# A streaming-encoder block on one core: the causal mask halved and moved into the opening's pool, its memory given to third places for three kinds of tiles

## The chip, the cores and the metric

The kernel runs on one core of one Trainium2 chip. The metric is the device time of one execution in microseconds (us): the median of three timed runs. TensorE does the matmuls, VectorE (DVE) and ScalarE (ACT) the work on elements, GpSimd (POOL) some more of it, and SyncE (SP) issues most of the transfers between HBM and the on-chip memory (SBUF). An engine works through its own instructions in order.

## The reference

One layer of a block with two branches, for 1,024 tokens of width 1,024, all in float32:

```
h = rmsnorm(x, ln1_g) * (1 + sc1) + sh1
q, k, v, cb, cc, cx, ga, gb = split(h @ w_in)          # eight sections of 1024 columns
q, k = rmsnorm(q per head), rmsnorm(k per head)        # 16 heads of 64
y_a = stick_breaking_attention(q, k, v)                # strictly causal
y_b = cb * causal_dwconv3(cc * cx)
merged = sigmoid(ga) * (y_a @ w_branch_a) + sigmoid(gb) * (y_b @ w_branch_b)
x = x + g1 * (merged @ w_out)
h = rmsnorm(x, ln2_g) * (1 + sc2) + sh2
x = x + g2 * ((silu(h @ w_ffn_gate) * (h @ w_ffn_up)) @ w_ffn_down)
```

sh1, sc1, g1, sh2, sc2 and g2 come from a small product of the condition c with `ada_w`.

## The kernel before

Every float32 operand of a large product is split into a high part (a copy in the fast matmul format) and a low part (the difference), and a product is three matmuls: high by high, high by low and low by high. So nearly each weight and each activation passes ScalarE (the copy) and VectorE (the subtraction) before TensorE reads it.

The stages, in the order of the program:

- **Opening** (L313 to L417). The modulation's sums, the squares of x, and the sections v (sweep `psr`) and again v with the modulation's shift (`pss`). TensorE first warms up with matmuls on the mask `mk` (L323 to L332). The sweep over k fills six PSUM banks for the first six token tiles; the last two tiles are done by `tail(k0, k1)`. `tail(0, KB)` runs ahead of `bcast` (L383), which spreads the rows' scales over all partitions by small matmuls, and `tail(KB, KT)` runs behind it. `bcast` writes into banks that `finish_raw(0)` and `finish_raw(1)` have emptied. From L169 to L496 the order on every engine is written out: `in_order` ties each instruction to the one before it on its engine. The opening's own pool `sp` is closed at L417, and the next pool, `ap`, begins at the same place in memory; its first tile, `vs`, is written by `finish_v(pss[0], 0)` (L480).
- **Keys and factors** (L420 to L614).
- **Gates** (L745 to L816). Twenty pairs of column blocks, each done with seven products in place of eight (`g_prod`, 12 matmuls each). For the first four pairs, the queries, a finished tile c goes through `put_q`: its high and low parts are stored, it is squared, and the square is split into `sh` and `sl` in a tile `sq2` of tag `sq`. `sum_q` then adds the squares up over partitions by two matmuls (L701). `later()` is called four times a pair, between two products, and decides when: it holds finished squares back in the list `pmm`. The modulation's later sums (`mods_later`) also load into tiles of tag `sq`.
- **Attention** (L977 to L1130), with TensorE's gaps filled by branch B's products (`fillers`). The order on TensorE, and of attention's own steps on VectorE and GpSimd, is tied. `load_sb` reads the gates of branch B into tiles of tag `sgi`.
- **Branch A** (L1167 to L1206). The attention's output is read into tiles `yr` (L1173) and split into `ya` (L1176, L1177). For each of 16 tiles there are 24 matmuls (`mm_ch`, L1026 to L1028) into one of two banks `pj`; the product is multiplied by the gate `sa` of tag `sgi` (loaded at L1192, used at L1197), `mb` is added (L1198), and the result is split (L1202, L1203). The gate's place is free when L1203 is done.
- **Output, second norm and the feed-forward part** (from L1213).

Where no order is tied, a planner that simulates the engines' times orders each engine's instructions and thus also the transfers that it issues. A tag with `bufs` places holds so many tiles; the next one waits until the oldest is no longer read. Pools on the left side of the memory stand on top of each other from `const` upwards.

The mask `mk` is a 128 x 1,024 tile in the pool `const`, which lives to the end: zeros, and in the last 128 columns ones on and above the diagonal (L88 to L91). Only the warming matmuls read its second half, `mr` copies it for them, and L497 stores 512 zeros of its first row into HBM, as the row ahead of the values `d_v[1]`.

Of the kernel before, what the change touches and what calls it, by code (L numbers as in the profile page):

```python
# [9 lines left out]
F32 = mybir.dt.float32  # L10
F32R = mybir.dt.float32r
AF = mybir.ActivationFunctionType
ALU = mybir.AluOpType
# [4 lines left out]
P = 128  # L18
T = 1024
D = 1024  # L20
# [10 lines left out]
def block_kernel(tc, x, x_t, cols, ada_1, ada_2, ada_row, w_q, w_kv, w_cg, w_a, w_b, w_o, w_g, w_u, w_d, out):  # L31
    nc = tc.nc
    st = ExitStack()
    const = st.enter_context(tc.tile_pool(name="const", bufs=1, reuse_waits="tile"))
# [5 lines left out]
    def nm(s):  # L40
        uid[0] += 1
        return f"{s}_{uid[0]}"
# [12 lines left out]
    def load_w(src):  # L55
# [14 lines left out]
    d_v = [drp.tile([n, P + 1, KT, P], F32, name=f"d_v{n}_{e}") for e, n in enumerate((4, 4))]  # L70
# [14 lines left out]
    ident = const.tile([P, P], F32, name="dm")  # L85
    make_identity(nc, ident)

    mk = const.tile([P, D], F32, name="mk")  # L88
    nc.gpsimd.memset(mk, 0.0)
    nc.gpsimd.affine_select(out=mk[:, D - P:], in_=mk[:, D - P:], compare_op=ALU.is_ge, fill=1.0, base=-1,  # L90
                            pattern=[[-1, P]], channel_multiplier=1)  # L91
    one = const.tile([P, 1], F32, name="one")
    nc.vector.memset(one, 1.0)
    nc.scalar.activation(one, one, AF.Silu)
# [75 lines left out]
    s1 = ExitStack()  # L170
    sp = s1.enter_context(tc.tile_pool(name="start", bufs=1, reuse_waits="tile"))
    xts = xp.tile([P, KT, T], F32, name="xts")

    def xt(k, n=None):
        ns = slice(0, T) if n is None else slice(n * 512, n * 512 + 512)
# [22 lines left out]
    def load_ada(m, k):  # L198
        ads[m, k] = load_ring(ada_1[k][:, m])

    wq = []
    NLD, MC, NW, KB = 5, 2, 3, 2

    def load_wq(qt):
        wp, bufs = wps
# [116 lines left out]
    load_x(3)  # L322
    warm = [ps_tr() for e in range(2)]  # L323
    for e in range(NW - 1):
        nc.tensor.matmul(warm[0], ident, mk[:, 512:], start=True, stop=True)
    mr = [sp.tile([P, n], F32R, name=nm("mr")) for n in (P, 512)]
    for m_ in mr:
        nc.scalar.activation(m_, mk[:, D - m_.shape[1]:], AF.Copy)
    for whole in (1, 1, 0, 0, 1, 1, 0, 1, 1, 1, 1):
        for e in range(2 - whole):  # L330
            r = slice(0, P) if whole else slice(64 * e, 64 * e + 64)
# [70 lines left out]
    for k in range(KT - 1):  # L402
        real(pss, k, range(MC), wq[4:])
        split_lo(k + 9)
        for n in range(2):
            make_hi(k + 1, n)
            make_lo(k + 1, n)
        if k + 2 < KT:
            split_hi(k + 10)
            shift_sum(k + 2)  # L410
            norm_x(k + 2)
        real(pss, k, range(MC, 8), wq[4:])
        if k % 2 == 0:
            load_wq(k // 2 + 6)
        if k + 3 < KT:
            load_ada(0, k + 3)
    s1.close()  # L417


# [74 lines left out]
            load_wq(9 + i // 2)  # L494
            split_w(9 + i // 2)
    ends = in_order(i0)  # L496
    nc.scalar.dma_start(d_v[1][:, 0:1, 0].rearrange("r p d -> p r d"), mk[0:1, :512].rearrange("p (r d) -> p r d", d=P))  # L497

    def put_before(e):

# [129 lines left out]
    def g_big():  # L630
        return gp.tile([P, T + 2], F32, tag="uu", bufs=2, name=nm("uu"))
# [28 lines left out]
    def mods_later():  # L660

        csb, cab = g_big()[:, :D], gp.tile([P, D], F32, tag="tr", bufs=2, name=nm("cab"))
        nc.scalar.dma_start(cab, ada_row[0:1, :].broadcast_to([P, D]))
        nc.scalar.activation(csb, cab, AF.Sigmoid)
        tt(nc.vector, cab, cab, csb, ALU.mult)
        yield

        def big_(i):
            tag = ("uu", "sq", "uu", "sq", "tr")[i % 5]
            return g_big()[:, :D] if tag == "uu" else gp.tile([P, D], F32, tag=tag, bufs=2, name=nm("ad"))  # L670

        yield from mod_sums((2, 4), big_, lambda s, t_: g_tile()[:, :P], cab, nc.scalar, g_ss)

# [11 lines left out]

    def put_q(c, m, n):

        sq2, hl_ = (gp.tile([P, 2, 512], F32R, tag=t_, bufs=2, name=nm("gt")) for t_ in ("sq", "tr"))
        hi, lo, sh, sl = hl_[:, 0], hl_[:, 1], sq2[:, 0], sq2[:, 1]
        nc.scalar.activation(hi, c, AF.Identity, scale=qgc)  # L690
        nc.vector.scalar_tensor_tensor(out=lo, in0=c, scalar=qgc, in1=hi.bitcast(F32), op0=ALU.mult, op1=ALU.subtract)
        nc.scalar.activation(c, c, AF.Square)
        nc.scalar.activation(sh, c, AF.Copy)
        tt(nc.vector, sl, c, sh.bitcast(F32), ALU.subtract)
        for e, t in ((0, hi), (1, lo)):
            nc.scalar.dma_start(d_q[e][m, :, n * 512:(n + 1) * 512], t.bitcast(F32))
        pmm.append((m, n, sh, sl))
# [47 lines left out]
    for g, (sec, j) in enumerate(gates):  # L745
        raw, raw2 = raws
        p1, p2 = pre[g] if g in pre else (g_prod(g_split(raw[:, :512]), 0), g_prod(g_split(raw[:, 512:]), 1))
        a11, a12, a21, a22 = raw[:, :512], raw[:, 512:], raw2[:, :512], raw2[:, 512:]
        s1, s2_, s3, s4 = (gp2.tile([P, 512], F32, tag=f"ws{q}", bufs=1, name=nm("ws")) for q in range(4))
        with tc.high_priority() if g == 0 else ExitStack():  # L750
            tt(nc.gpsimd, s3, a11, a21, ALU.subtract)
            tt(nc.gpsimd, s2_, a22, s3, ALU.subtract)
            w6 = g_split(s2_)
        tt(nc.gpsimd, s1, a21, a22, ALU.add)
        ws4 = nc.gpsimd.tensor_tensor(out=s4, in0=a12, in1=s2_, op=ALU.subtract)
        if g + 1 < len(gates):
            raws = two_raw(g + 1)
        c11, c21, c12, c22 = (gp.tile([P, 512], F32, tag=f"c{q}", bufs=2, name=nm("c")) for q in range(4))

        def put(c, m, n):  # L760
            if sec == 5:
                pend.append((c, m, n))
            elif sec > 2:
                nc.scalar.activation(c, c, AF.Sigmoid)
                nc.scalar.dma_start((d_sga, d_sgb)[sec - 3][m, :, n * 512:(n + 1) * 512], c)
            elif sec == 1:
                ccs[m, n] = c
            elif n == 1 and m >= 4:
                ccs["late"] = c
            else:  # L770
                put_u(c, m, n)
                if n == 0 and m >= 4:
                    put_u(ccs["late"], m, 1)

        def later():
            if len(pmm) > 1 or pmm and not pend:
                sum_q(*pmm.pop(0))
            if pend:
                put_q(*pend.pop(0))
            elif g > 3 and not pmm:  # L780
                with tc.issue_after(ws4.ins):
                    next(eq, None)

        nc.scalar.activation(c11, p1, AF.Copy)
        p4 = g_prod(g_split(a22), 3) if g + 1 == len(gates) else None
        p6 = g_prod(w6, 5)
        tt(nc.vector, c21, p6, c11, ALU.add)
        tt(nc.vector, c11, p2, c11, ALU.add)
        put(c11, j, 0)
        later()  # L790
        p5 = g_prod(g_split(s1), 4)
        tt(nc.vector, c12, p5, c21, ALU.add)
        p3 = g_prod(g_split(s4), 2) if g == 0 else None
        p7 = g_prod(g_split(s3), 6)
        tt(nc.vector, c22, p7, c12, ALU.add)
        put(c22, j + 4, 1)
        later()
        tt(nc.vector, c21, p7, c21, ALU.add)
        p3 = p3 or g_prod(g_split(s4), 2)
        tt(nc.vector, c12, p3, c12, ALU.add)  # L800
        put(c12, j, 1)
        later()
        p4 = p4 or g_prod(g_split(a22), 3)
        tt(nc.vector, c21, p4, c21, ALU.add)
        later()
        put(c21, j + 4, 0)
        if g + 1 == len(gates):
            for _ in eq:
                pass
        for _ in range((3 if sec in (3, 4) else 0) if g + 1 < len(gates) else 50):  # L810
            next(ml, None)
# [218 lines left out]
    def fillers():  # L1030
# [19 lines left out]
            nc.sync.dma_start(d_yb[1][n][:, m, :], yl.bitcast(F32))  # L1050
            yield 0.65 * KQ
        def load_sb(m, n):
            sb = fp.tile([P, 512], F32, tag="sgi", bufs=2, name=nm("sgi"))
            nc.sync.dma_start(sb, d_sgb[m, :, n * 512:(n + 1) * 512])
            return sb

# [112 lines left out]
    yah, yal = ([[None] * KT for n in range(2)] for e in range(2))  # L1169
    with tc.high_priority():  # L1170
        for (tag, bufs), (n, k) in zip(slots, [(0, k) for k in range(7)] + [(1, 0), (1, 1), (1, 2), (0, 7)] + [(1, k) for k in range(3, 8)]):
            yr = fp.tile([P, 512], F32, tag="yr", bufs=2, name=nm("yr"))
            nc.sync.dma_start(yr, d_ya[n][:, k, :])  # L1173
            ya2 = bp.tile([P, 2, 512], F32R, tag=tag, bufs=bufs, name=nm("ya"))
            h_, l_ = ya2[:, 0], ya2[:, 1]
            nc.scalar.activation(h_, yr, AF.Copy)  # L1176
            tt(nc.vector, l_, yr, h_.bitcast(F32), ALU.subtract)  # L1177
            yah[n][k], yal[n][k] = h_, l_
    mh, mlo = [None] * 2, [None] * 2
    wa = {}  # L1180
    for it, (m, n) in enumerate([(0, 0), (1, 0), (0, 1), (1, 1)] + [(m, n) for m in range(2, KT) for n in range(2)]):
# [6 lines left out]
        if (m, n) == (KT - 1, 0):  # L1188
            with tc.issue_after(last_m.ins):
                preload_wo()  # L1190
        sa = fp.tile([P, 512], F32, tag="sgi", bufs=2, name=nm("sgi"))
        nc.sync.dma_start(sa, d_sga[m, :, n * 512:(n + 1) * 512])  # L1192
        mb = fp.tile([P, 512], F32, tag="st", bufs=3, name=nm("mb"))
        nc.sync.dma_start(mb, d_mb[m, :, n * 512:(n + 1) * 512])
# [596 lines left out]
```

## Time and profile before

| | |
|---|---|
| timed runs | 1797.07 us median (1796.59 to 1797.15, 3 runs) |
| the profiled execution | 1798.88 us, its span 1796.9 us |
| TensorE busy | 1784.6 us, 99% of the span |
| VectorE, ScalarE, GpSimd busy | 1272.0, 830.8, 342.9 us |
| moved by transfers | 359.09 MB, 200 GB/s on average |

A profile is one execution on the chip. A row of a timeline gives the start and the length in us, the engine, the source line, what is written and read, the shape, a count of like instructions, and in brackets how long the engine stood idle before it and what ended that. `L137` is the line of a helper, so its rows are told apart by their tiles. Matmuls are pipelined: a row's length is that of one matmul from its start to its end, and the next one starts before that. An engine named with a q (SPq, ACTq) is its sequencer, issuing a transfer. The granted clock is the share of TensorE's full clock that the throttle let through.

### The profile page before, as it was taken

To read this page: it belongs to the slowest core of one execution; us is meant where nothing else is said; L and a number is where in the kernel's file an instruction comes from. 1 tells how busy PE (TensorE), PEld (TensorE's weight loads), DVE (VectorE), ACT (ScalarE), POOL (GpSimd) and SP (SyncE) were. 2 spreads that over 40 slices of the span, in tenths; PEclk is the share of its full clock that TensorE was granted. 3 is DMA by queue.
4 is the path that set the end of the run, shared out by engine and by line. 5 is a ranking of instruction groups with operands and counts; after the bars stand their busy time and mean duration, and the time that the engine had idled before them with its cause. 6 is when DMAs were issued, how large, how long until landed. Compare 5 with 4: busy or idle time off the path is not lost.

```text
span 1796.9 us, 24937 instructions
## 1 busy us (share of the span) xinstructions
PE 1784.6 (99%) x8611; PEld 1486.4 (83%) x8611; DVE 1272.0 (71%) x2030; ACT 830.8 (46%) x1555; POOL 342.9 (19%) x437
## 2 busy tenths in 40 slices
PE   9999999999999999999999999999999999999999
PEld 7888877888888888888888788888888888888887
DVE  6876576777774678777786764698867786644776
ACT  5534364333433567766675221764544454432321
POOL 0024334723231233333342100100000000000000
PEclk9999999999999999999999999999999999999999
DMA  9469654222644977796656766334533444389776
GB/s 384 165 237 382 239 187 141 88 87 99 222 151 143 297 193 189 207 320 179 169 135 199 263 210 213 129 104 157 220 130 134 159 171 159 136 320 348 272 235 222
DMA packets 165010, 359.09 MB, mean 200 GB/s; under 512 B 15538, under 2 KB 60938, under 8 KB 163732
## 3 DMA queue, kind: packets, MB, share of 16 engines
q1 hardware_dynamic: 128300, 289.65, 48.8%
q10 hardware_dynamic: 33096, 55.25, 8.7%
q0 software_dynamic: 3488, 12.59, 2.1%
q8 instruction: 69, 1.13, 0.3%
q14 instruction: 57, 0.47, 0.1%
HBM read 247.84 MB, written 109.62 MB: 199 GB/s over the span
## 4 chain that ended last, share of the span: by engine, by line
PE 93%; DMA 3%; DVE 2%; ACT 1%; issue 1%; POOL 0%; SPq 0%; ACTq 0%; DVEq 0%; POOLq 0%
PE e L133 8%; PE e L131 8%; PE e L132 8%; PE pj L133 7%; PE pj L131 7%; PE pj L132 7%; PE pj L294 7%; PE pj L1026 4%; PE pj L1027 4%; PE pj L1028 4%; PE e L1619 4%; PE e L1618 4%; PE e L1620 4%; PE tr L950 3%; PE o L966 2%; PE z L921 2%
## 5 line engine op out<-in xcount | busy, mean ns | idle before, releaser
L1234 ACT ACTIVATE whi<-raw 128x512 fp32r<-128x512 f32 x137 | 85.0, 628 | 160.8 <-PE e L132 101.8
L1235 DVE TENSOR_TENSOR wlo<-raw,whi 128x512 fp32r<-128x512 f32 x137 | 93.2, 687 | 71.0 <-ACT whi L1234 53.5
L137 POOL TENSOR_TENSOR pt<-pt 128x63 f32<-128x63 f32 (+7 forms) x128 | 101.8, 795 | 211.7 <-DVE pt L936 188.8
L132 PE MATMUL e<-big,whi 128*128 128x512 f32 x352 | 136.9, 389 | 0.0
L131 PE MATMUL e<-big,whi 128*128 128x512 f32 x352 | 136.5, 390 | 0.0
L133 PE MATMUL e<-big,wlo 128*128 128x512 f32 x352 | 136.1, 389 | 0.0
L294 PE MATMUL pj<-whi,big 128*128 128x512 f32 x448 | 132.6, 393 | 0.5 <-ACT big L263 0.3
L137 DVE TENSOR_TENSOR c<-pj,c 128x512 f32<-128x512 f32 x140 | 93.5, 683 | 50.7 <-PE pj L133 50.2
L954 DVE TENSOR_TENSOR atl<-tr,ath 128x512 fp32r<-128x512 f32 (+1 forms) x192 | 104.0, 553 | 34.3 <-ACT ath L953 33.0
L131 PE MATMUL pj<-big,whi 128*128 128x512 f32 x320 | 125.0, 391 | 0.0
L133 PE MATMUL pj<-big,wlo 128*128 128x512 f32 x320 | 124.8, 390 | 0.0
L132 PE MATMUL pj<-big,whi 128*128 128x512 f32 x320 | 124.6, 389 | 0.0
L1619 PE MATMUL e<-wlo,f 128*128 128x512 f32 (+1 forms) x319 | 121.8, 382 | 0.0
L1618 PE MATMUL e<-whi,f 128*128 128x512 f32 (+1 forms) x319 | 121.6, 382 | 0.0
L1620 PE MATMUL e<-whi,f 128*128 128x512 f32 (+1 forms) x319 | 121.6, 382 | 0.0
L923 ACT ACTIVATE pt<-z,rq 128x128 f32<-128x128 f32 (+1 forms) x192 | 107.3, 579 | 26.3 <-PE z L922 23.3
L1026 PE MATMUL pj<-big,whi 128*128 128x512 f32 x256 | 113.2, 442 | 0.0
L137 DVE TENSOR_TENSOR wlo<-raw,whi 128x512 fp32r<-128x512 f32 x108 | 87.3, 813 | 32.4 <-ACT whi L524 32.1
L524 ACT ACTIVATE whi<-raw 128x512 fp32r<-128x512 f32 x108 | 67.3, 628 | 90.0 <-PE pj L132 51.5
L953 ACT ACTIVATE ath<-tr 128x512 fp32r<-128x512 f32 (+1 forms) x192 | 93.3, 489 | 28.5 <-PE tr L950 27.4
L131 PE MATMUL e<-rh,whi 128*128 128x512 f32 x264 | 102.7, 389 | 0.0
L132 PE MATMUL e<-rl,whi 128*128 128x512 f32 x264 | 102.7, 389 | 0.0
(304 smaller groups left out, 4760.4 us busy)
## 6 DMA issues: line engine op xcount, KB each, us to landing
f<-d_f SPq DMA_DIRECT2D x77, 512.0 KB, 4.4
d_f<-fs SPq DMA_DIRECT2D x70, 512.0 KB, 3.2
raw<-w_cg SPq DMA_DIRECT2D x40, 512.0 KB, 3.7
raw<-w_u SPq DMA_DIRECT2D x26, 512.0 KB, 4.2
raw<-w_g SPq DMA_DIRECT2D x25, 512.0 KB, 4.0
raw<-w_kv SPq DMA_DIRECT2D x20, 512.0 KB, 5.0
ld<-ada SPq DMA_DIRECT2D x16, 512.0 KB, 6.6
d_t<-ts SPq DMA_DIRECT2D x16, 512.0 KB, 6.9
```

The source lines that it names most:

```text
L131: nc.tensor.matmul(ps, wh[:, k, :], fh[:, k, :], start=(k == 0 and not onto), stop=False, skip_group_check=onto)
L132: nc.tensor.matmul(ps, wh[:, k, :], fl[:, k, :], start=False, stop=False, skip_group_check=onto)
L133: last = nc.tensor.matmul(ps, wl[:, k, :], fh[:, k, :], start=False, stop=(k == 3), skip_group_check=onto)
L137: eng.tensor_tensor(out=out, in0=a, in1=b, op=op)
L294: nc.tensor.matmul(ps, a, b, start=(k == 0 and q == 0), stop=(k == KT - 1 and q == 2))
L923: nc.scalar.activation(pt[:, off + s0:off + s0 + m], z[:, :m], AF.Sigmoid, scale=rq[:, 1, i, h:h + 1])
L953: nc.scalar.activation(th[:, :nb, c0:c0 + P], src, AF.Copy)
L954: nc.vector.tensor_tensor(out=tl[:, :nb, c0:c0 + P], in0=src, in1=th[:, :nb, c0:c0 + P].bitcast(F32), op=ALU.subtract)
L1026: nc.tensor.matmul(ps, wh, rh_, start=(k == 0), stop=False)
L1618: nc.tensor.matmul(o, sh, w[0][:, c], start=(j == 0), stop=False)
L1619: nc.tensor.matmul(o, sh, w[1][:, c], start=False, stop=False)
L1620: nc.tensor.matmul(o, sl, w[0][:, c], start=False, stop=(j == NJ - 1))
```

## The change

The mask leaves `const`, is 512 columns wide, and is made in the opening's pool `sp`; the zero row is stored at the end of the opening, before the pool closes, and so inside the stretch whose order is tied. `const` is 4 KB a partition smaller. That memory goes to a third place for tiles of tag `sq` (4 KB) in the gates' pool, and later to a third place each for `sgi` and `yr` (2 KB each) in the pool `fp`. Two counts change with it: `KB` is 3, so `tail` does three steps of k ahead of the broadcast, and `later()` holds squares back until more than two are waiting.

```
-    mk = const.tile([P, D], F32, name="mk")
-    nc.gpsimd.memset(mk, 0.0)
-    nc.gpsimd.affine_select(out=mk[:, D - P:], in_=mk[:, D - P:], compare_op=ALU.is_ge, fill=1.0, base=-1,
-                            pattern=[[-1, P]], channel_multiplier=1)
...
+    mk = sp.tile([P, 512], F32, name="mk")
+    nc.gpsimd.memset(mk, 0.0)
+    nc.gpsimd.affine_select(out=mk[:, 512 - P:], in_=mk[:, 512 - P:], compare_op=ALU.is_ge, fill=1.0, base=-1,
+                            pattern=[[-1, P]], channel_multiplier=1)
...
-    NLD, MC, NW, KB = 5, 2, 3, 2
+    NLD, MC, NW, KB = 5, 2, 3, 3
...
-        nc.tensor.matmul(warm[0], ident, mk[:, 512:], start=True, stop=True)
+        nc.tensor.matmul(warm[0], ident, mk, start=True, stop=True)
...
+    nc.scalar.dma_start(d_v[1][:, 0:1, 0].rearrange("r p d -> p r d"), mk[0:1].rearrange("p (r d) -> p r d", d=P))
     s1.close()
...
     ends = in_order(i0)
-    nc.scalar.dma_start(d_v[1][:, 0:1, 0].rearrange("r p d -> p r d"), mk[0:1, :512].rearrange("p (r d) -> p r d", d=P))
...
-            return g_big()[:, :D] if tag == "uu" else gp.tile([P, D], F32, tag=tag, bufs=2, name=nm("ad"))
+            return g_big()[:, :D] if tag == "uu" else gp.tile([P, D], F32, tag=tag, bufs=3 if tag == "sq" else 2, name=nm("ad"))
...
-        sq2, hl_ = (gp.tile([P, 2, 512], F32R, tag=t_, bufs=2, name=nm("gt")) for t_ in ("sq", "tr"))
+        sq2, hl_ = (gp.tile([P, 2, 512], F32R, tag=t_, bufs=b_, name=nm("gt")) for t_, b_ in (("sq", 3), ("tr", 2)))
...
-            if len(pmm) > 1 or pmm and not pend:
+            if len(pmm) > 2 or pmm and not pend:
                 sum_q(*pmm.pop(0))
...
-            sb = fp.tile([P, 512], F32, tag="sgi", bufs=2, name=nm("sgi"))
+            sb = fp.tile([P, 512], F32, tag="sgi", bufs=3, name=nm("sgi"))
...
-            yr = fp.tile([P, 512], F32, tag="yr", bufs=2, name=nm("yr"))
+            yr = fp.tile([P, 512], F32, tag="yr", bufs=3, name=nm("yr"))
...
-        sa = fp.tile([P, 512], F32, tag="sgi", bufs=2, name=nm("sgi"))
+        sa = fp.tile([P, 512], F32, tag="sgi", bufs=3, name=nm("sgi"))
```

More of the change, by code (lines that the diff above doesn't have):

```diff
@@ L324, in block_kernel @@
     for e in range(NW - 1):
-        nc.tensor.matmul(warm[0], ident, mk[:, 512:], start=True, stop=True)
+        nc.tensor.matmul(warm[0], ident, mk, start=True, stop=True)
     mr = [sp.tile([P, n], F32R, name=nm("mr")) for n in (P, 512)]
     for m_ in mr:
-        nc.scalar.activation(m_, mk[:, D - m_.shape[1]:], AF.Copy)
+        nc.scalar.activation(m_, mk[:, 512 - m_.shape[1]:], AF.Copy)
     for whole in (1, 1, 0, 0, 1, 1, 0, 1, 1, 1, 1):
```

## The prediction

> **What bounds the kernel now.** I read the page first: its busy shares and its chain that ended last.
>
> ```profile
> span 1796.9 us, 24937 instructions
> ...
> PE 1784.6 (99%) x8611; PEld 1486.4 (83%) x8611; DVE 1272.0 (71%) x2030; ACT 830.8 (46%) x1555; POOL 342.9 (19%) x437
> ...
> PE 93%; DMA 3%; DVE 2%; ACT 1%; issue 1%; POOL 0%; SPq 0%; ACTq 0%; DVEq 0%; POOLq 0%
> ```
>
> TensorE is busy for 99% of the span and carries 93% of the chain. The change leaves every matmul as it is, so it can win only where TensorE stands still. The view of waits, for TensorE alone, lists those places (us in total, times, longest):
>
> ```profile
> PE tr L325 <- POOL mk L90: 2.5, 1, 2.5
> PE pj L1026 <- DVE sgi L1197: 2.0, 1, 2.0
> PE tr L701 <- DVE gt L137: 1.3, 1, 1.3
> PE pj L258 <- ACT vs L310: 1.0, 1, 1.0
> ```
>
> The rows below these add up to 1.8 us. So at most about 9 us can be had at all, and the change names a tile of each of these four rows. What lies between them is full, by the windows (length, then busy time of PE, PEld, DVE, ACT, POOL with their instructions, then the granted clock, the DMA share and GB/s):
>
> ```profile
> 57.80:96.00 38.20, 38.20 (x170) 31.65 (x169) 31.37 (x42) 16.48 (x29) 0.00 (x0) 1.00 0.49 166
> 262.00:590.00 328.00, 328.00 (x1451) 269.54 (x1451) 232.63 (x336) 123.44 (x205) 120.94 (x81) 1.00 0.41 137
> 600.00:980.00 380.00, 378.60 (x2331) 328.94 (x2330) 294.90 (x503) 262.81 (x585) 144.21 (x259) 1.00 0.74 207
> 1013.60:1019.00 5.40, 5.34 (x17) 4.25 (x18) 5.30 (x10) 1.15 (x2) 0.84 (x2) 0.68 0.57 190
> ```
>
> 170 matmuls in 38.20 us is a pitch of 0.225 us. The fourth row is another thing: 17 matmuls in 5.40 us at a mean granted clock of 0.68, where 17 x 0.225 = 3.8 us would do. Some 1.6 us are lost right behind the longest wait, in busy time that no list of waits shows.
>
> **Part A, three steps of the tail ahead of the broadcast (KB 2 to 3).**
>
> ```profile
> 46.29 0.39 PE L294 MATMUL tr<-whi,big 128*128 128x512 f32 x1
> 47.72 2.05 PE L258 MATMUL pj<-dm,rs_r 128*128 128x128 f32 x16 [1.04 <-ACT vs L310]
> ```
>
> From start to start that is 1.43 us, of which 0.23 is the pitch: 1.20 us lost. One more k puts 2 x 3 = 6 matmuls there, 6 x 0.225 = 1.35 us, so the broadcast starts about 0.15 us later than now and no longer waits. The six are missing behind it, so the end of the tail comes 1.20 us earlier. Behind it stand:
>
> ```profile
> 53.46 1.42 DVE L281 SCALAR_TENSOR_TENSOR big<-xts,mod,big 128x512 fp32r<-128x512 f32 x2 [1.20 <-ACT big L277]
> ```
>
> ```profile
> 57.80 0.62 PE L294 MATMUL pj<-whi,big 128*128 128x512 f32 x2
> ```
>
> The first product of the next sweep would start at 56.6 us; its lower halves are ready at 54.88, with the later broadcast at 55.03, so 1.6 us are left. The banks that the sweep takes later are emptied when the tail is done, so they follow TensorE. Nothing new is late. Gain 1.20; if that cover were gone, 0.15 less. This stretch has its order on every engine fixed by the program, so the planner moves nothing.
>
> **Part B, squares summed one turn later (len(pmm) > 2, third place for sq).**
>
> ```profile
> 258.09 0.39 PE L132 MATMUL pj<-big,whi 128*128 128x512 f32 x1
> 259.74 0.41 PE L701 MATMUL tr<-gt,sel 128*16 128x512 f32 x1 [1.26 <-DVE gt L137]
> ```
>
> ```profile
> 258.40 0.68 DVE L137 TENSOR_TENSOR wlo<-ws,whi 128x512 fp32r<-128x512 f32 x1
> 259.00 0.68 DVE L137 TENSOR_TENSOR gt<-c,gt 128x512 fp32r<-128x512 f32 x1
> ```
>
> The sum waits for the lower half of the squares, which VectorE makes right behind another tile, without a pause. Lost: 1.65 - 0.225 = 1.42 us. A turn is a product of 12 matmuls, 2.7 us, so a sum that comes one turn later finds its operand ready; the weights that the next matmuls read (the wlo of 258.40) are done before 259.1. Gain 1.42, and 32 sums stay 32. The last sum also comes a turn later; what hangs on it (the rows rq) is wanted by attention some 300 us on. This stage is ordered by the planner, which will order it anew. Bounds: a new order can leave the same 1.42 us in another place (gain 0), or lose as much again (-1.42), and with the 328.00 us busy of 328.00 it can't gain more. I take 1.42.
>
> **Part C, third places for sgi and yr.**
>
> ```profile
> 1011.29 0.39 PE L1028 MATMUL pj<-ya,wlo 128*128 128x512 f32 x1
> 1013.66 0.47 PE L1026 MATMUL pj<-ya,whi 128*128 128x512 f32 x1 [1.99 <-DVE sgi L1197]
> ```
>
> ```profile
> 1002.49 0.69 DVE L1197 TENSOR_TENSOR sgi<-pj,sgi 128x512 f32<-128x512 f32 x1 [1.77 <-DMA sgi<-d_sga]
> ...
> 1005.38 0.69 DVE L1203 TENSOR_TENSOR big<-sgi,big 128x512 fp32r<-128x512 f32 x1
> ...
> 1012.83 0.69 DVE L1197 TENSOR_TENSOR sgi<-pj,sgi 128x512 f32<-128x512 f32 x1 [4.16 <-DMA sgi<-d_sga]
> ```
>
> ```profile
> 1006.10 0.32 SPq L1192 DMA_DIRECT2D sgi<-d_sga x1
> ```
>
> The load of 1006.10 is issued 0.03 us after L1203 of 1005.38 gave its place back (1005.38 + 0.69), and takes 6.7 us to the multiplication at 1012.83; the bank that this one empties is what TensorE waits for. With three places the load waits for the L1203 one tile earlier, by at least the 5.4 us that a tile's 24 matmuls take: issued by 1000.7, landed by 1007.4. VectorE stood ready at 1008.67 (1012.83 less the 4.16 of its wait), so L1197 ends at 1009.4, ahead of the 1011.5 at which TensorE asks. The start-to-start loss, 2.37 - 0.225 = 2.14 us, goes, and with it the slow matmuls, 1.6 us: 3.74 in this execution. What could be late next is the other operand mb, which has three places already. The third yr only takes waiting from ACT that TensorE doesn't see. Bounds: nothing (SP issues in order, and an older load could hold the new one back), and 3.74.
>
> [...]
>
> **Part D, the mask.**
>
> ```profile
> 0.86 0.95 POOL L89 MEMSET mk<- 128x1024 f32 x1
> ```
>
> ```profile
> 5.25 4.91 PE L332 MATMUL tr<-mr,mr 128*128 128x512 f32 x14
> 10.50 1.66 PE L294 MATMUL pj<-whi,big 128*128 128x512 f32 x6 [0.34 <-ACT big L263]
> ```
>
> Half the memset saves about 0.48 us on GpSimd, and the warming matmuls start as much earlier. The first real ones at 10.50 wait for loaded data, so the gap ahead of them grows from 0.34 to about 0.8 us and nothing is won: 0.
>
> ```profile
> 2.48 1.16 ACTq L497 DMA_DIRECT2D d_v<-mk x1
> ...
> 86.85 1.34 ACT L277 ACTIVATE big<-xts,mod 128x512 fp32r<-128x512 f32 x2 [0.96 <-DVE xts L272]
> ...
> 96.76 0.60 ACT L484 ACTIVATE vs<-pj 128x512 f32<-128x512 f32 x1 [4.95 <-PE pj L294]
> ```
>
> The store of the zero row moves from 2.48 to behind ACT's 86.85, 1.16 us of issue. Queued behind it are the splits of two weights and then L484, which stood idle for 4.95 us and whose tile takes the mask's place, so it now also waits for the landing. With the 6.7 us of the load above, the longest row here, that is 88.2 + 1.2 + 6.7 = 96.1, before 96.76. Cost 0; if a landing took longer, each us beyond shows on ACT first.
>
> **The sum.** The profiled execution took 1798.88 us, 1.98 around its span. Removed: 1.20 + 1.42 + 3.74 = 6.36, so 1792.5. The median of the timed runs, 1797.07, lies 1.81 us under the profiled one. That is about the 1.6 us of slow clock, and I take it that the timed runs mostly lack it. For them: 1.20 + 1.42 + 2.14 = 4.76 us, 1797.07 - 4.8 = 1792.3 us. A measurement of this kernel tells 0.2%, 3.6 us, from no change: the limits are 1793.5 and 1800.7.
>
> **The rivals.**
> 1. *The slow clock is in the timed runs too.* Then 6.4 us go: 1790.7. For it, the matmuls themselves show it in the one trace; against it, the 1.81 us. Chance 0.12.
> 2. *Only A and B come, the third wait moves on.* SP's queue is in order, and if the planner puts the new load behind another that waits, L1197 is late as before: 1.20 + 1.42 = 2.6, 1794.5. Part of B given back lands here too, down to A and nothing else, 1795.9. For it: two of three stages are planned anew. Chance 0.20.
> 3. *The opening goes cold.* The warming ends 0.48 us earlier, and the idle stretch before 10.50 drops the clock as it did at 1013. The price is that row's 1.6 us, and with A's wait filled nothing absorbs it: 4.8 - 1.6 = 3.2, 1793.9. For it: the drop behind 1.99 us idle. Against: 0.8 us is less than the 1.26 us at 259 that brought no drop that the windows show. Chance 0.05. [...]
> 4. *It doesn't do what it says.* The waits are latencies of data and not of places: 1797.1. The 0.03 us between L1203 and the load speak against it. Chance 0.05.
> 5. *Slower: ACT stops in the tail of attention.* The splits of yr go ahead of other work there, and ACT works in order. A third place lets the planner put one more split in front before its data is in.
>
> ```profile
>   DMA yr<-d_ya: 7.4, 4
> ...
> DMA to landing us min/median/max: 2.8/4.0/4.1
> ```
>
> ACT has already waited 7.4 us in 4 such waits, while TensorE lost nearly nothing. If such waits reach TensorE, each costs up to 4.0 us; from the second on the gain is gone (8.0 > 4.8), and with three it is 1797.07 - 4.8 + 12.0 = 1804.3. Against it: another place lets a load start earlier. Chance 0.10.
>
> **How the numbers follow.** Forecast 0.48, rivals 0.12, 0.20, 0.05, 0.05, 0.10. Faster by over 0.2%: the forecast but for a tail of 0.04 that loses over 1.2 us on the way, and rival 1: 0.56. Same: that tail, rivals 2, 3 and 4 and the lighter part (0.01) of rival 5: 0.35. Slower: 0.09. The range, 1790.2 to 1797.3, leaves out rival 5 alone: its lower end is rival 1 with the other 0.5 us of the small waits, its upper end rival 4 with a little scatter.
>
> **What would show it.** Right: in the waits of TensorE the rows of L258, L701 and L1026 are gone or under 0.3 us; the granted clock is 1.00 around 1010; the first row is about 2.0 in place of 2.5; the broadcast starts near 47.9; the first sgi loads lie one tile ahead. Wrong: an L1026 or an L950 row of over 1 us at 930 to 1015, a new row of 1 us between 180 and 310, or a granted clock under 1 at 10 to 14 us.

## The result, and the profile after

The kernel after took 1793.22 us in the median of 14 runs (1792.38 to 1794.68), the kernel before 1797.62 us in 14 runs beside them (1796.26 to 1799.31): a ratio of 0.9976, with a 95% interval of 0.9967 to 0.9984. That is 4.40 us less, of 4.76 forecast. The profiled execution took 1792.41 us against 1798.88, 6.47 less, of 6.36 forecast. A later set of 11 runs (e9 below) gave 0.9979 (0.9970 to 0.9988), 3.84 us less. One run of the kernel before beside e5 to e8 took 2216.55 us at a mean granted clock of 0.753, and is left out of every number below.

The page of the kernel after, its span, busy shares and chain that ended last:

```profile
span 1790.4 us, 24937 instructions
...
PE 1782.5 (100%) x8611; PEld 1485.4 (83%) x8611; DVE 1273.5 (71%) x2030; ACT 830.9 (46%) x1555; POOL 345.0 (19%) x437
...
PE 96%; DMA 1%; DVE 1%; issue 0%; ACT 0%; POOL 0%; SPq 0%; POOLq 0%; DVEq 0%; ACTq 0%
```

The instructions are as many as before; TensorE's part of the chain went from 93% to 96%, and DMA's from 3% to 1%. The waits of TensorE in the kernel after (us in total, times, longest):

```profile
PE tr L325 <- POOL mk L171: 2.0, 1, 2.0
PE tr L950 <- POOL pt L133: 0.9, 2, 0.5
PE pj L294 <- ACT big L263: 0.4, 1, 0.4
```

The rows of L701 and L1026, 1.3 and 2.0 us, are gone. (Helpers stand four lines higher now: L137 is L133.) The timeline of the kernel after around the broadcast, and the start of the next sweep:

```profile
47.50 0.39 PE L294 MATMUL tr<-whi,big 128*128 128x512 f32 x1
48.14 2.05 PE L258 MATMUL pj<-dm,rs_r 128*128 128x128 f32 x16 [0.25 <-ACT vs L310]
...
54.59 1.42 DVE L281 SCALAR_TENSOR_TENSOR big<-xts,mod,big 128x512 fp32r<-128x512 f32 x2 [1.91 <-ACT big L277]
...
56.85 0.61 PE L294 MATMUL pj<-whi,big 128*128 128x512 f32 x2
```

The broadcast still waits 0.25 us, and the next sweep starts 0.95 us earlier (57.80 before). Branch A in the kernel after, the multiplication by the gate and the windows (length, busy time of PE, PEld, DVE, ACT, POOL with instructions, granted clock, DMA share, GB/s):

```profile
1003.54 0.69 DVE L1197 TENSOR_TENSOR sgi<-pj,sgi 128x512 f32<-128x512 f32 x1 [1.17 <-PE pj L1028]
1008.98 0.69 DVE L1197 TENSOR_TENSOR sgi<-pj,sgi 128x512 f32<-128x512 f32 x1 [0.94 <-PE pj L1028]
```

```profile
262.00:590.00 328.00, 328.00 (x1453) 269.66 (x1452) 229.96 (x333) 121.62 (x201) 121.84 (x81) 1.00 0.41 138
...
1013.60:1019.00 5.40, 5.40 (x26) 4.46 (x25) 3.89 (x7) 1.15 (x2) 0.74 (x2) 1.00 0.84 306
```

L1197 waited for a DMA before (4.16 us at 1012.83); now it waits for TensorE's product, as it should where TensorE is the bound. The load of the gate that is multiplied at 1008.98 is the second of this row on SP's queue, issued at 998.3:

```profile
997.10 1.52 SPq L1192 DMA_DIRECT2D sgi<-d_sga  x2
```

So it comes 10.7 us ahead of its reader, in place of the 6.7 us before. In the second window stand 26 matmuls at a clock of 1.00 where 17 at 0.68 had been.

To compare kernels beyond one execution I cut each profile at the same four events on TensorE: the first product of the next sweep after the broadcast (L294), the first matmul of attention that writes z (L921), the first matmul that reads ya (L1026 to L1028), and the first one behind the last that reads it. Lengths in us, from start to start; the opening counts from the start of the span. All profiles of the study are in this table, with what each keeps of the change:

| profile | KB | squares | sgi | yr | opening | to attention | attention | branch A |
|---|---|---|---|---|---|---|---|---|
| before | 2 | as before | 2 | 2 | 57.80 | 541.01 | 364.52 | 106.60 |
| e1, before again | 2 | as before | 2 | 2 | 58.31 | 540.27 | 364.36 | 107.64 |
| e4, mask alone | 2 | as before | 2 | 2 | 57.82 | 539.73 | 365.90 | 105.60 |
| e10, sgi alone | 2 | as before | 3 | 2 | 58.08 | 539.61 | 364.34 | 102.70 |
| e8, KB as before | 2 | changed | 3 | 3 | 58.06 | 539.21 | 365.97 | 102.75 |
| e5, squares as before | 3 | as before | 3 | 3 | 56.83 | 539.74 | 365.35 | 102.70 |
| e6, place of sq alone | 3 | place only | 3 | 3 | 56.72 | 539.92 | 363.96 | 102.70 |
| e7, later turn alone | 3 | turn only | 3 | 3 | 56.92 | 539.87 | 364.99 | 102.70 |
| after | 3 | changed | 3 | 3 | 56.85 | 539.21 | 364.54 | 102.70 |
| e9, after again | 3 | changed | 3 | 3 | 56.76 | 539.26 | 365.96 | 102.75 |
| e3, yr as before | 3 | changed | 3 | 2 | 56.62 | 539.21 | 364.03 | 102.75 |
| e12, four steps, yr as before | 4 | changed | 3 | 2 | 56.63 | 539.91 | 364.94 | 102.74 |
| e2, sgi as before | 3 | changed | 2 | 3 | 56.54 | 539.21 | 366.05 | 108.93 |
| e11, sgi and yr as before | 3 | changed | 2 | 2 | 57.77 | 539.92 | 365.06 | 105.26 |

In the first pair of profiles the columns account for the gain: 0.95 + 1.80 - 0.02 + 3.90 = 6.63, less 0.12 that the stretch from branch A to the last matmul is longer: 6.51, of 6.52 us of span. The other rows say which of these numbers belong to the kernel and which to one execution.

### The profile page after: what moved, and what is told of

Same layout as the page of the kernel before. It is cut to its first block, busy times and chain, and to the rows that moved or that the text cites. A ratio compares the mean times of both kernels' runs of the same rounds, so it can differ in the third digit from the quotient of the medians.

```text
span 1790.4 us, 24937 instructions
## 1 busy us (share of the span) xinstructions
PE 1782.5 (100%) x8611; PEld 1485.4 (83%) x8611; DVE 1273.5 (71%) x2030; ACT 830.9 (46%) x1555; POOL 345.0 (19%) x437
## 3 DMA queue, kind: packets, MB, share of 16 engines
q8 instruction: 69, 1.13, 0.3%
## 4 chain that ended last, share of the span: by engine, by line
PE 96%; DMA 1%; DVE 1%; issue 0%; ACT 0%; POOL 0%; SPq 0%; POOLq 0%; DVEq 0%; ACTq 0%
PE e L129 8%; PE e L128 8%; PE e L127 8%; PE pj L127 7%; PE pj L128 7%; PE pj L129 7%; PE pj L294 7%; PE pj L1026 5%; PE pj L1028 5%; PE pj L1027 5%; PE e L1618 4%; PE e L1619 4%; PE e L1620 4%; PE tr L950 3%; PE o L966 2%; PE z L921 2%
## 5 line engine op out<-in xcount | busy, mean ns | idle before, releaser
L133 POOL TENSOR_TENSOR pt<-pt 128x63 f32<-128x63 f32 (+7 forms) x128 | 101.6, 794 | 212.1 <-DVE pt L936 195.7
L294 PE MATMUL pj<-whi,big 128*128 128x512 f32 x448 | 132.6, 393 | 0.6 <-ACT big L263 0.4
L133 DVE TENSOR_TENSOR c<-pj,c 128x512 f32<-128x512 f32 x140 | 93.7, 684 | 53.9 <-PE pj L129 53.3
L524 ACT ACTIVATE whi<-raw 128x512 fp32r<-128x512 f32 x108 | 67.5, 629 | 109.0 <-PE pj L128 54.3
L133 DVE TENSOR_TENSOR wlo<-raw,whi 128x512 fp32r<-128x512 f32 x108 | 89.4, 831 | 36.2 <-ACT whi L524 36.1
L1026 PE MATMUL pj<-big,whi 128*128 128x512 f32 x256 | 113.3, 442 | 0.0
```

Source lines behind the costliest of these rows:

```text
L133: eng.tensor_tensor(out=out, in0=a, in1=b, op=op)
L294: nc.tensor.matmul(ps, a, b, start=(k == 0 and q == 0), stop=(k == KT - 1 and q == 2))
L1026: nc.tensor.matmul(ps, wh, rh_, start=(k == 0), stop=False)
```

## The experiments

My theory after the result: each part removed the wait that the prediction named. The rivals: the new order of the planned stages, or the scatter of single executions, did it.

**e1, the kernel before once more**, with no edit.

> The kernel before, unchanged, to see the granted clock of each single run. Its 14 runs so far fall into two groups, seven at 1796.3 to 1797.2 us and seven at 1798.1 to 1799.3, about 1.9 us apart. Theory A: the upper group is the runs in which one window of TensorE, 3.41 us long, ran at half clock behind the 1.99 us wait near 1013; it loses 1.7 us. Then the runs with a mean clock of 0.999 (1 - 0.5 x 3.41 / 1797 = 0.99905) are the upper group and those with 1.000 the lower one, with no run in the wrong group. Theory B: the spread has another cause (transfers, the chip's clock): both clocks occur in both groups.

Its 11 runs had a median of 1797.03 us, and 31 runs of the kernel before on the same chip 1797.17. With more runs the two groups fill up to one spread from 1795.0 to 1799.8, so the clean split of theory A is wrong; its size, 1.7 us, is near. In all 107 runs of the kernel before in three sets, 63 had a mean granted clock of 1.000 and a mean time of 1796.59 us, 43 had 0.999 and 1798.59: 2.0 us more, in two runs of five. One more had 0.998 and 1800.68. That the 0.999 stands for a slow window behind L1026 is seen in two of these runs, the profiled ones (before and e1). The mean also counts a half clock behind the last matmul, where it costs nothing (0.9 us in the profile of before, 1.7 in e5's), so it is not a sure sign. The waits of TensorE in e1's profile show how far one execution is from the next:

```profile
PE pj L1026 <- DVE sgi L1197: 3.0, 1, 3.0
PE tr L325 <- POOL mk L90: 2.5, 1, 2.5
PE pj L258 <- ACT vs L310: 1.4, 1, 1.4
PE tr L950 <- POOL pt L137: 0.7, 2, 0.4
```

L1026 now 3.0 us, and no row of L701 at all, in the same kernel.

**e2, two places for sgi**, the rest of the change kept:

```
-            sb = fp.tile([P, 512], F32, tag="sgi", bufs=3, name=nm("sgi"))
+            sb = fp.tile([P, 512], F32, tag="sgi", bufs=2, name=nm("sgi"))
...
-        sa = fp.tile([P, 512], F32, tag="sgi", bufs=3, name=nm("sgi"))
+        sa = fp.tile([P, 512], F32, tag="sgi", bufs=2, name=nm("sgi"))
```

> The kernel after with two places for the gate tiles of tag sgi again, and everything else of the change kept. Theory A: the third sgi place alone removed the stall near 1013. Then the L1026 row of about 2.0 us is back in TensorE's waits and the time is 2.1 us over the kernel after, or 3.8 in runs in which the clock also drops: about 1795.4 to 1797.0, some 2.2 to 0.6 under the kernel before. Theory B: the third place of yr, or the planner's new order of the stage, removed it: no L1026 row over 0.3 us, and the time stays at 1793.2, 4.4 under the kernel before.

1799.61 us in the median of 11 runs, against 1797.17: ratio 1.0014 (1.0005 to 1.0023). The stall is back, so theory B falls; but it came back threefold, and the time missed the 1795.4 to 1797.0 of theory A on the slow side. The waits of TensorE in e2:

```profile
PE pj L1026 <- DVE sgi L1197: 3.7, 3, 1.8
```

SP's queue in e2, and in e11 (two places for yr as well, below):

```profile
997.71 0.32 SPq L1194 DMA_DIRECT2D mb<-d_mb  x1
998.31 1.52 SPq L1192 DMA_DIRECT2D sgi<-d_sga  x2
1000.52 0.33 SPq L513 DMA_DIRECT2D raw<-w_a  x1
1009.33 2.67 SPq L1194 DMA_DIRECT2D mb<-d_mb  x2
```

```profile
1006.11 0.32 SPq L1192 DMA_DIRECT2D sgi<-d_sga  x1
1006.72 0.33 SPq L513 DMA_DIRECT2D raw<-w_a  x1
1007.32 0.32 SPq L1194 DMA_DIRECT2D mb<-d_mb  x1
1008.71 0.32 SPq L1192 DMA_DIRECT2D sgi<-d_sga  x1
```

In e2 the planner put the gate loads in pairs: each of the two is issued in the moment in which an L1203 gives a place back, and the next pair comes 14 us later. In e11 they alternate with loads of mb. Such a pair stands in all seven profiles with three places for yr and in none of the seven with two; with three places for sgi it stands once, and TensorE does not wait for it.

**e3, two places for yr** (`yr = fp.tile(...)` with `bufs=2`):

> The kernel after with two places for branch A's inputs of tag yr again. Theory A: they only take waiting from ACT that TensorE does not see; ACT waits some 7 us for these transfers again in place of 1.1, and the time stays within 0.3 us of the kernel after (4.4 under the kernel before). Theory B: they had a share in the 3.9 us that the trace shows gone near 1013: an L1026 row over 0.3 us is back and the time rises by 0.5 to 3.8.

1792.12 us (9 runs) against 1797.17: ratio 0.9971 (0.9962 to 0.9981), 5.05 less. No row of L1026, branch A at 102.75: theory A, but for the time, which is 0.65 us better than the 4.40 of the kernel after, in place of 0.3, and within its interval. ACT's waits are back, and no cost of them is seen; the waits of ACT in e3:

```profile
ACT ya L1176 <- DMA yr<-d_ya: 7.8, 4, 3.0
```

**e4, the mask's part alone**: KB 2, `len(pmm) > 1`, and two places for sq, sgi and yr.

> The mask's part alone: the kernel after with two places for sq, sgi and yr, squares held back until more than one waits, and two steps of the tail ahead of the broadcast, as in the kernel before. Theory A (the prediction's part D): costs and wins nothing, within 0.5 us of the kernel before; the three waits of L258, L701 and L1026 are all there with 1.0, 1.3 and 2.0 us. Theory B: the shorter memset counts for the time, which starts 0.4 us earlier with TensorE's first matmul: 0.4 us under the kernel before. Theory C: the moved store of the zero row, or the other addresses of the tiles, cost something that the other parts of the change hide: over 0.5 us slower.

1797.06 us (11 runs) against 1797.17: ratio 1.0001 (0.9992 to 1.0010). Nearest to theory A. The interval is 1.6 us to each side, so the 0.4 us of theory B and a small cost by theory C are not excluded by the time; the opening of 57.82, against 57.80 and 58.31 in before and e1, shows nothing of theory B. Of the three waits two are in its profile (L258 1.0 us, L1026 2.6 us), the one of L701 is not.

**e5, the squares as before**, **e6, the place alone**, **e7, the later turn alone**. e5 has both of these edits to the kernel after, e6 the first alone, e7 the second alone.

```
-            if len(pmm) > 2 or pmm and not pend:
+            if len(pmm) > 1 or pmm and not pend:
```

```
-            return g_big()[:, :D] if tag == "uu" else gp.tile([P, D], F32, tag=tag, bufs=3 if tag == "sq" else 2, name=nm("ad"))
+            return g_big()[:, :D] if tag == "uu" else gp.tile([P, D], F32, tag=tag, bufs=2, name=nm("ad"))
...
-        sq2, hl_ = (gp.tile([P, 2, 512], F32R, tag=t_, bufs=b_, name=nm("gt")) for t_, b_ in (("sq", 3), ("tr", 2)))
+        sq2, hl_ = (gp.tile([P, 2, 512], F32R, tag=t_, bufs=b_, name=nm("gt")) for t_, b_ in (("sq", 2), ("tr", 2)))
```

> The kernel after with part B undone: squares held back until more than one waits, two places for sq. Theory A: the L701 row of 1.3 us is back, one stall of 1.4 us start to start between 180 and 310 us, and the time is 1.4 us over the kernel after (3.0 under the kernel before where the kernel after is 4.4 under it). Theory B: the stall went by the new order of the stage (sgi, mask's memory) and not by B: no L701 row, time as the kernel after.

> The kernel after with the third place of sq, but squares held back only until more than one waits, as before. Theory A (the turn cures the stall, since the sum waited for VectorE's subtraction and not for a place): the L701 row of 1.3 us is back and the time is 1.4 us over the kernel after. Theory B (the place cures it): no L701 row, time as the kernel after.

> The kernel after with squares held back until more than two wait, but two places for sq. Theory A (the turn alone would do, the place only keeps it legal and easy): no L701 row over 0.3 us, time within 0.4 us of the kernel after. Theory B (with three squares waiting and two places, the third waits for a place): ScalarE and VectorE are held at L690 and its neighbours until a sum has freed one, the products' banks are emptied late and TensorE loses 1 us or more between 180 and 310.

Against 1797.43 us of the kernel before beside them (32 runs): e5 1794.30, ratio 0.9983 (0.9974 to 0.9992); e6 1793.77, 0.9984 (0.9975 to 0.9993); e7 1793.62, 0.9982 (0.9973 to 0.9991); 11 runs each (the ratios are estimates of their own, not quotients of the medians). None of the three profiles shows the stall of 1.4 us (0.2 us are left in e6, and e5 has no row of L701), so theory A of e5 and e6 misses, and B of e5 fits the profile; e7 fits its theory A. But e4, e10 and the kernel before itself in e1 have the old squares too, and none of them shows it. It belongs to one execution. What made it there is seen on GpSimd, which sums the weights. The best profile to compare is e4's: its opening is as long (57.82 us, 57.80 in the first profile of before) and its squares are summed as before. GpSimd in the first profile of before; then GpSimd, VectorE and TensorE in e4:

```profile
250.96 1.30 POOL L137 TENSOR_TENSOR ws<-raw,raw 128x512 f32<-128x512 f32 x1 [15.23 <-DMA raw<-w_q]
```

```profile
248.95 1.57 POOL L133 TENSOR_TENSOR ws<-raw,raw 128x512 f32<-128x512 f32 x1 [13.46 <-DMA raw<-w_q]
...
257.73 0.68 DVE L133 TENSOR_TENSOR gt<-c,gt 128x512 fp32r<-128x512 f32 x1
...
258.45 0.40 PE L701 MATMUL tr<-gt,sel 128*16 128x512 f32 x1
```

In both GpSimd waited for the weights' transfer. It was issued at 245.5 us in the first and at 245.2 in e4, and took 5.4 us to GpSimd's start against 3.8, so GpSimd began 2.0 us later. The split of these weights stands right ahead of the squares on VectorE. They are done at 259.00 + 0.68 = 259.68 in the first and at 257.73 + 0.68 = 258.41 in e4: 1.27 us later, and the sum is 1.29 us later. In e1, the same kernel as the first:

```profile
258.54 0.68 DVE L137 TENSOR_TENSOR gt<-c,gt 128x512 fp32r<-128x512 f32 x1
...
259.52 0.40 PE L701 MATMUL tr<-gt,sel 128*16 128x512 f32 x1
```

There the squares are done at 259.22, 0.46 us earlier than in the first, and TensorE comes to the sum 1.05 us later, at 259.52, as its opening was 0.5 us longer and it had waited elsewhere: so no stall.

**e8, two steps ahead of the broadcast** (`KB` 2 in place of 3):

> The kernel after with part A undone: two steps of the tail ahead of the broadcast. Theory A: the L258 row of 1.0 us is back, the next sweep starts at 57.8 in place of 56.6 to 56.9, and the time is 1.2 us over the kernel after, or 0.8 by the one execution in which 0.41 us of the wait was left. Theory B: what is won ahead of the broadcast is lost behind it in most runs (the margin of L281 before the next sweep shrank to 0.8 us): time as the kernel after.

1795.61 us (11 runs) against 1797.43: ratio 0.9988 (0.9979 to 0.9997), 1.82 less. The opening is 58.06 long, and the waits of TensorE have the row again:

```profile
PE pj L258 <- ACT vs L310: 1.4, 1, 1.4
```

Theory A. The 2.4 us to the 1793.22 of the kernel after is more than the 1.2 expected; within the intervals, and e8's profile has stalls of its own elsewhere: from branch A to the last matmul it takes 724.40 us, and 723.07 to 723.66 in all others.

**e9, the kernel after again**, with no edit.

> The kernel after, unchanged, on one chip with the next three, and a second profile of it. Theory A (the mechanisms of the parts hold, and what differed between profiles is scatter of single executions): 4.0 to 5.0 us under the kernel before; the opening's wait of L258, 0.25 us in the first profile, is under 0.3; no row of L701 or L1026; granted clock 1.00 around 1010. Theory B (the first profile of after was a lucky one): a stall of over 1 us stands in the gates or in branch A, and the time is less than 3.5 under the kernel before.

1793.46 us (11 runs) against 1797.30 (33 runs): ratio 0.9979 (0.9970 to 0.9988). Theory A, but for the size: 3.84 less, a little under its 4.0. No row of L258, L701 or L1026.

**e10, the third place of sgi alone** (the kernel after with KB 2, `len(pmm) > 1`, and two places for sq and yr):

> The third place of sgi alone (with the mask moved, which makes the room): yr and sq with two places, squares held back until more than one waits, two steps of the tail ahead. Theory A (the third place of sgi carries the change): branch A without a stall and without slow clock; the profiles of kernels with two places lost 2.15, 3.17 and 2.81 us there, and 17 of 42 runs of the kernel before show a mean clock of 0.999 and are 1.7 us slower, so 2.7 + 0.4 x 1.7 = 3.4 us under the kernel before. Theory B (by the prediction's sum): 2.1 under it. Theory C (parts A and B carry as much of the change as the sum says): under 2.

1794.31 us (11 runs): ratio 0.9984 (0.9975 to 0.9993), 3.0 us less. Nearest to theory A's 3.4; the interval, 1.3 to 4.5 us, can't exclude B or C. The profile can say more: branch A takes 102.70 us, as in all nine profiles with three places, and 105.26 to 108.93 in the five with two. L1197 in e10:

```profile
1004.97 0.69 DVE L1197 TENSOR_TENSOR sgi<-pj,sgi 128x512 f32<-128x512 f32 x1 [0.65 <-PE pj L1028]
1010.41 0.69 DVE L1197 TENSOR_TENSOR sgi<-pj,sgi 128x512 f32<-128x512 f32 x1 [0.94 <-PE pj L1028]
```

**e11, two places for sgi and for yr**, A and B kept:

> The kernel after with two places for sgi and two for yr, parts A and B kept. The same with three places for yr was 2.4 us slower than the kernel before (1799.6 against 1797.2), with three waits of L1026. Theory A (with two places for sgi, a third yr makes the planner put loads in an order that costs): one L1026 wait of 2 to 3 us as in the kernel before, and the time is 1.0 to 2.4 us under the kernel before (A and B alone). Theory B (parts A and B themselves shift the stage into a worse order): as slow as with three places for yr, 1 us or more over the kernel before.

1797.03 us (11 runs): ratio 0.9999 (0.9990 to 1.0008). One wait of 2.2 us and not the 3.7 us in three of e2, so the order that e2 got comes with the third yr, and theory B falls. But A and B left only 0.3 us, under theory A's 1.0 to 2.4. Eight of the 11 runs have a clock under 1.000, two of them 0.998. The three with 1.000 have a mean of 1794.71 us, against 1796.57 in the 20 such runs of the kernel before beside them: 1.9 less, so what A and B won was lost to the clock in most runs, as far as three runs can tell. Its profile shows where a window was slow: not in branch A, in spite of the wait, but in the opening. TensorE's timeline and the windows in e11:

```profile
4.83 3.94 PE L332 MATMUL tr<-mr,mr 128*128 128x512 f32 x14
10.66 2.08 PE L294 MATMUL pj<-whi,big 128*128 128x512 f32 x6 [1.89 <-ACT big L263]
```

```profile
10.60:15.10 4.50, 4.44 (x13) 3.49 (x13) 4.45 (x8) 2.48 (x5) 0.00 (x0) 0.62 1.00 382
```

The full clock came early in this run (at 4.86 us, in the first profile of after at 7.57), the warming matmuls ended at 8.77, and 1.89 us idle followed. The opening took 57.77 in place of 56.5 to 56.9.

**e12, four steps ahead of the broadcast and two places for yr**, for a version that beats both:

> A version that may beat the kernel after: four steps of the tail ahead of the broadcast in place of three, and two places for yr in place of three (which was 1.1 us faster by its median, within the scatter between chips). Theory A: in executions where ACT's release comes late (48.14 in the first profile of after), the fourth step fills up to 0.25 us of the wait; with the third place of yr gone 0.3 to 1.0 us under the kernel after of the same chip. Theory B: the six matmuls more ahead of the broadcast push it 1.35 us later where nothing waits, L281 ends as much later, its margin of 0.6 to 1.1 us before the next sweep is gone and TensorE waits there: 0.3 to 0.7 us over the kernel after. Theory C: the same time within 0.3 us.

1793.28 us (11 runs) against e9's 1793.46 on the same chip: theory C, the same time. In e2, e3 and e9 the broadcast has no wait over 0.2 us with three steps, so the fourth finds nothing to fill. No version here is shown to beat the kernel after: e3's 1792.12 us is 1.1 us lower, but its gain is within the interval of the kernel after.

## Why the prediction was right, and where its sizes were off

The forecast (1792.3) and the side (faster) came out, the mechanism of A and C as given; the size of B did not, and that the sum came within 0.4 us is in part luck.

**A** was 1.20. In the first pair of profiles it was 0.95: there ACT's release L310 came at 47.42 in place of 47.00, after a longer wait for x, and 0.25 us of the wait were left. Over the table, the five profiles with KB 2 have a mean opening of 58.01 us, the eight with more steps and no slow clock there one of 56.73: 1.28. The cover held, but by less than was counted: L281 began 1.13 us later than before (54.59 against 53.46) and not 0.15, and ends at 54.59 + 1.42 = 56.01, 0.84 ahead of the next sweep in place of 1.6.

**B** was 1.42, and this is the step that failed. It rested on "the sum waits for the lower half of the squares, which VectorE makes right behind another tile": true of that execution, but the six other profiles that lack B or a half of it (e1, e4, e5, e6, e7, e10) have no such stall. Their way to attention takes 539.61 to 540.27 us, where 539.21 to 539.26 stand in five of the seven profiles with all of B. In the other two, e11 and e12, and in e1 and e7, it holds a wait for L524 shortly behind 220 us, ahead of the sum at 259: 0.4 us, and 0.3 in e7. It is this row in the waits of TensorE in e1:

```profile
PE pj L131 <- ACT whi L524: 0.4, 1, 0.4
```

So B is worth 0.4 to 0.5 us in most executions (539.61 to 539.74 in e4, e5 and e10 against 539.2), and 1.8 in the one that the prediction read. The later turn runs with two places as well (e7). With the waits for L524 taken out, from start to start 0.6 us, e7's 539.87 is 539.3, near the kernel after, while e6 with the place alone takes 539.92, no less than with the old squares. So the turn seems to be the half that counts; one profile of each does not prove it.

**C** was 2.14, or 3.74 with the clock. In the first pair it was 3.90. Over the profiles the wait with two places is 2.0, 3.0, 2.6 and 2.2 us (before, e1, e4, e11), so branch A is 2.6 to 4.9 us longer than with three; e10 measured 3.0 for it alone. The load's place was the cause, as the 0.03 us between L1203 and the load had said, and sgi's alone: with it, yr does nothing that is seen (e3, e12).

**D** was 0, and e4 shows no other size: TensorE's first matmul starts at 2.03 in place of 2.46, and the first real one of the kernel after at 10.40 against 10.50. The gap ahead of it, of which 0.8 us had been counted, is 0.42 in the first profile of after, 1.47 in e5, 1.60 in e9 and 1.89 in e11; rival 3 below is about that. The store of the zero row lies at 87.25 on ACT's queue, and L485, which is the old L484, waits for TensorE as before:

```profile
87.25 1.17 ACTq L417 DMA_DIRECT2D d_v<-mk  x1
...
95.81 0.60 ACT L485 ACTIVATE vs<-pj 128x512 f32<-128x512 f32 x1 [3.68 <-PE pj L294]
```

**The step from the profiled to the timed runs** was that these "mostly lack" the slow clock. By the mean clock three of five lack it (e1); the others are 2.0 us slower. With the sizes measured since, the sum is 1.28 for A, 0.4 for B, 2.6 for C's wait (2.15, 3.17, 2.81 and 2.39 from start to start less the pitch in before, e1, e4 and e11; their mean) and 0.4 x 2.0 = 0.8 at most for its clock, since 5 of 25 runs of the kernel after have 0.999 too: 4.3 to 5.1. So B was 1.0 too large and C 0.5 to 1.3 too small, and the two errors largely cancel. Measured were 4.40 and 3.84, with intervals of some 1.5 us to each side. What is left is inside the scatter of attention, whose length differs by 1.4 us between two profiles of the same kernel (364.54 and 365.96). The gain of the timed runs is thus not resolved into parts better than that.

**The rivals.** 1 is right in about two runs of five, by the mean clock. 2 did not come. 3 exists: in e11 the opening went cold behind 1.89 us idle, and cost 57.77 - 56.73 = 1.0 us. What decides in these profiles is how early the full clock comes: the first product starts at 10.4 to 10.7 us in all 14, and the warming, the same matmuls in each, ends the sooner the earlier they run at full clock: the 14 of L332 take 3.94 us in e11 and 5.15 in the first profile of after. The full clock came at 4.86 us in e11, 5.33 in e9 and 5.37 in e5 (gaps of 1.89, 1.60 and 1.47 us), and at 6.71 or later in the others (gaps of 0.9 us at most). Where it comes before the warming, the warming's start, 0.43 us earlier with the new mask, should make the gap longer by as much, an estimate; in the first pair the gap grew by 0.08. Whether it happens in runs of the kernel after, or of before, no profile shows. 4 fell. 5 did not come in the kernel after, but a third yr did harm with two places for sgi: e2 against e11, 2.6 us, where the rows point to SP's order of loads and not to ACT.

## What to carry to other kernels

A loss read off one execution is a loss of that execution until a second profile of the same kernel shows it: the wait that hung on when a transfer landed, of L701, was 1.3 us in one of seven profiles and at most 0.2 in the six others; the wait that hung on a place came in all five profiles without it. A place was worth 3.0 us (e10) where a load was issued in the moment in which another was given back and was late for its reader; with the third sgi every profile had the same branch A to 0.05 us, so here the place also took the scatter away. And an added place changes the order in which a planner issues loads: one that does nothing by itself (yr) cost some 2.6 us where the scarce one (sgi) was missing.

## What the runs showed of the hardware

In the profile of before the trace's records of the granted clock begin with the full clock at 7.42 us; it is 0.50 from 1014.36 for 3.413 us, full again from 1017.77, and 0.50 from 1796.01 to the end. From start to start the matmuls of branch A take 0.43 us in that half step and 0.225 ahead of the wait. In the profile of after the record is full from 7.57 to 1789.32. The full stretches of the two are 1006.93, 778.24 and 1781.76 us long: 295, 228 and 522 times 3.4133. So in each of these two profiles the records change on a grid of 3.413 us. Its offset is not the same in each: the full clock came at 7.42 us in before, 7.57 in after, 5.33 in e9 and 4.86 in e11. Where no record marks an edge, it is counted from one that does in steps of 3.4133 us, an estimate. Idle stretches (from a matmul's end to the next start) and the step of the grid that holds them, in us:

| profile | line after the gap | idle | within the grid's step | clock behind it |
|---|---|---|---|---|
| before | L1026 | 1011.67 to 1013.66: 1.99 | 1010.94 to 1014.36, all | half, 1014.36 to 1017.77 |
| e1 | L1026 | 1011.28 to 1014.29: 3.01 | 1011.19 to 1014.61, all | half from 1014.61 |
| e2 | L1026 | 1004.71 to 1006.47: 1.76 | 1004.23 to 1007.64, all | half from 1007.64 |
| e11 | L294 | 8.77 to 10.66: 1.89 | 8.27 to 11.68, all | half from 11.68 |
| e4 | L1026 | 1011.79 to 1014.43: 2.64 | 1.94 before the edge at 1013.73, 0.70 behind it | full |
| e11 | L1026 | 1011.11 to 1013.33: 2.22 | 0.68 before the edge at 1011.79, 1.54 behind it | full |
| e9 | L294 | 9.01 to 10.61: 1.60 | 8.74 to 12.16, all | full |

Behind 1.76 us inside one step (e2) the clock was half, behind 2.64 us over two steps (e4) it was full. The windows of e4 behind its gap, 25 matmuls at full clock, against 18 in 5.70 us of e1:

```profile
1014.40:1020.00 5.60, 5.57 (x25) 4.65 (x26) 5.50 (x10) 1.15 (x2) 1.05 (x2) 1.00 0.56 192
```

```profile
1014.30:1020.00 5.70, 5.70 (x18) 4.56 (x19) 5.60 (x10) 1.15 (x2) 1.05 (x2) 0.70 0.55 180
```

The 18 matmuls of e1 are 7 fewer, 7 x 0.225 = 1.6 us, and half a step is 1.7 us. So the same wait cost its length in one run (e4) and its length and some 1.6 us in another (e1); in the six rows of over 1.7 us this goes by whether the gap lies inside one step. The 2.0 us between the two groups of e1 are a little more than the 1.7 us of half a step, and what makes the rest stays open. Inside one step 1.76 us (e2), a little over its half, had a half clock behind it, and 1.60 us (e9) had not. The 1.94 us that e4 had on one side of an edge left the clock full too, so the time within a step does not order all seven rows; this stays open.
